# A one-core hybrid decoder layer: the w_o projection with the tokens stationary, its gate and x loaded as rows in its first slab, and five spare buffers for modulation weights in two more stretches

## The chip, the cores and the metric

The kernel runs on one core of one Trainium2 chip. A core has a matrix engine (TensorE, PE in the profile, with its weight loads shown apart as PEld), a vector engine (VectorE, DVE), a scalar engine (ScalarE, ACT), GpSimd (POOL) and SyncE (SP), whose queue issues nearly all DMAs here. The metric is the device time of one execution in microseconds (us), lower is better. The kernel before was timed three times: 1594.55, 1594.61 and 1588.14 us, median 1594.55.

## The reference

One layer (depth 1) for 256 tokens of width 2048, all in float32:

```python
mod = (silu(c) @ ada_w[l] + ada_b[l])[:, None, :]
sh1, sc1, g1, sh2, sc2, g2 = split(mod, 6)              # each 2048 wide
h = modulate(rms_norm(x, norm1_g[l]), sh1, sc1)         # h * (1 + scale) + shift
u, lru_gate, q, k, v, mix_gates = split(h @ w_in[l] + b_in[l])
y_lru  = rg_lru(conv(u)) * gelu(lru_gate)               # 16 heads of 128
y_attn = sliding_window_attention(q, k, v, sinks)       # window 128, 16 q heads, 4 kv heads
merged = sigmoid(g_A) * (y_lru @ w_lru_out[l]) + sigmoid(g_B) * (y_attn @ w_attn_out[l])
x = x + g1 * (merged @ w_o[l])                          # the step that is changed
h2 = modulate(rms_norm(x, norm2_g[l]), sh2, sc2)        # and this one
gate, up = split(h2 @ w_ffn_in[l])                      # 2 x 5632
x = x + g2 * ((silu(gate) * up) @ w_ffn_out[l])
return rms_norm(x, final_g)
```

There is one vector c for all tokens, so each of the six parts of `mod` is one row of 2048 numbers. `ada_w` is 2048 x 12288, 100 MB in float32, a quarter of all that is read.

## The kernel before

**Products.** Every large product is float32 made of three fp32r products (`mm3`, lines 320 to 322): each weight and each activation is cut into a high part (`hi`, fp32r) and the rest (`lo`), and hi·hi, hi·lo and lo·hi are added up in PSUM. Weights come in items of 128 x 1024 (512 KB). An item is loaded by SP into one of five `raw` buffers (line 266), cast to `hi` by ScalarE (line 275, four buffers), and `lo = raw - hi` is made by VectorE (line 287, three buffers). Eight items are a slab: all 2048 input rows by 512 output columns. `step` (line 298) writes item after item: first the post work of finished slabs, then the load of item i+5, `hi` of i+3, `lo` of i+2, the loads of modulation weights, the products of item i, and then side work (lru, attention, modulation) as far as a planner's clock lets it.

**Two forms of a slab** (line 324, `add_slab`). With the weights stationary (`in_rows=False`), one item is 24 matmuls whose moving operand is 256 tokens; the result stands turned, features on the partitions. With the tokens stationary (`in_rows=True`), it is 12 matmuls whose moving operand is 512 weight columns; the result stands in rows, tokens on the partitions. The slabs come in this order: `wi` (u, gate, k, v, q; 14 slabs in pieces), `wgl` (4), `wl` (4), `wga` (4), `wa` (4), `wo` (4), then `fg`/`fu` (11 pairs) and the last product `pf`/`pl`. Only `wi` (but for v) and `wo` have the weights stationary.

**Modulation weights.** Shift, scale and gate 1 and shift and scale 2 are computed by VectorE as dot products (line 407): 158 loads of 512 KB (`aw<-in_ada_t_dram`, line 378), each multiplied by the row `crow` and added up into one column of `modc`, so `modc` holds them turned (128 x 16 for each part). Gate 2 is summed in rows during the first FFN slabs (line 595, 32 loads `aw<-in_ada_g_dram`). `Halves.fetch` has two buffers of its own for these loads (`N_ADA` = 2); when both are taken it may use one of the 25 general buffers `b4` if `spare()` allows. `spare` allows up to five (`N_SPARE`) at the start, and none from the last piece of `wi` on. SP's queue runs in the order in which it was written: a load of modulation weights that waits for its buffer holds all loads behind it.

**w_o and the second norm.** `o_post` adds gate 1 times the product to a turned copy of x (four loads `x1T`, line 120, issued after the first slab), squares it on ScalarE and sums it over features on VectorE. After the fourth slab `second_norm` (line 969) adds up the squares over partitions with ones as weights, takes root and reciprocal over 128 x 256, turns x into rows (32 transposes, line 956), copies the rows out of PSUM on ScalarE and stores them to DRAM (`x1d`, for the last residual), and makes `h2` pair by pair: scaled on VectorE (1001), high part on ScalarE (1005), low part on VectorE (1011).

Of the kernel before, what the change touches and what calls it, by code (L numbers as in the profile page):

```python
# [47 lines left out]

N_PIECES, N_F, K_FIRST = 3, 4, 2
# [16 lines left out]
def hybrid_layer(  # L66
    ctx: ExitStack, tc, vecs, x_t, ada_k, ada_t, ada_g, w_in, bv_row, bm_row, bg_row, lru_w, w_lru, w_att, w_o,
# [37 lines left out]
    def rows(t):  # L105
        return slice(t * P, (t + 1) * P)
# [807 lines left out]
    x1T, second = [], {}  # L914

    def o_post(s):
        def post(banks):
            if s == 0:
                x1T.extend(load_x("x1T"))
                second["fs"] = b4("fs2")  # L920
# [5 lines left out]
            yield 0, 0  # L926
            for f in range(4):
                xf = x1T[s][:, f, :]
                nc.vector.scalar_tensor_tensor(
                    xf, banks[f // 2][:, f % 2, :], modc[:, 2, 4 * s + f:4 * s + f + 1], xf,  # L930
                    op0=ALU.mult, op1=ALU.add,
                )
            yield 1.3, 0
            sq = b4(f"sq{s}")
            nc.scalar.activation(sq, x1T[s], AF.Square)
            yield 0, 0.95
            nc.vector.tensor_reduce(second["fs"][:, s, :], sq.rearrange("p k s -> p s k"), axis=AX.X, op=ALU.add)
            yield 1.14, 0
# [10 lines left out]
    pts = {}  # L949

    def rows_of(i, of_w=False):

        s, t = divmod(i, 2)
        pt = wtile(f"ptx{i}").rearrange("p j n -> p (j n)") if of_w else mtile(f"ptx{i}")
        for j in range(4):
            nc.tensor.transpose(pt[:, j * P:(j + 1) * P], x1T[s][:, j, rows(t)], ident)
        pts[i] = (pt, 0 if of_w else 1)

    def rows_out(i):
        s, t = divmod(i, 2)  # L960
        pt, m = pts.pop(i)
        xr = b4(f"xr{i}", F32, (512,))
        nc.scalar.copy(xr, pt)
        nc.sync.dma_start(x1d[rows(t), s * 512:(s + 1) * 512], xr)
        free(b4=1, m=m)
# [3 lines left out]
    def second_norm(banks):  # L969
        sides[:] = [ada_ffn]  # L970
        fs = second["fs"]
        both = h2["both"] = hp.tile([P, NK, 2, S], F32R, tag="h", name="h2_both")
        hh, hl = both[:, :, 0, :], both[:, :, 1, :]
        ps = mtile("r2_ps")[:, 0:S]
        for s in range(3):
            nc.tensor.matmul(ps, lhsT=ones, rhs=fs[:, s, :], start=s == 0, stop=False, skip_group_check=True)
        sq = b4("sq3")
        for f in range(4):
            xf = x1T[3][:, f, :]
            nc.vector.scalar_tensor_tensor(  # L980
                xf, banks[f // 2][:, f % 2, :], modc[:, 2, 12 + f:13 + f], xf, op0=ALU.mult, op1=ALU.add
            )
            nc.scalar.activation(sq[:, f, :], xf, AF.Square)
        for f in range(4):
            nc.tensor.matmul(ps, lhsT=ones, rhs=sq[:, f, :], start=False, stop=f == 3, skip_group_check=True)
        r2 = b4("r2")[:, 0, :]
        nc.scalar.activation(r2, ps, AF.Sqrt, bias=eps_t, scale=1.0 / D)
        nc.vector.reciprocal(r2, r2)
        free(m=1)

        for i in range(6):
            rows_of(i, i in (3, 4))
        for i in range(4):
            rows_out(i)
            if i < 2:
                rows_of(6 + i)

        def scaled(p):
            for kt in (2 * p, 2 * p + 1):
                xk = x1T[kt // 4][:, kt % 4, :]  # L1000
                nc.vector.scalar_tensor_tensor(xk, xk, modc[:, 4, kt:kt + 1], r2, op0=ALU.mult, op1=ALU.mult)

        def high(p):
            for kt in (2 * p, 2 * p + 1):
                nc.scalar.activation(
                    hh[:, kt, :], x1T[kt // 4][:, kt % 4, :], AF.Identity, bias=modc[:, 3, kt:kt + 1]
                )
# [379 lines left out]
```

## Time and profile before

| what | us |
|---|---|
| three runs | 1594.55, 1594.61, 1588.14 |
| median | 1594.55 |
| the profiled execution | 1595.45 |
| its span, first to last instruction | 1593.7 |
| PE busy in the span | 1568.6 |
| DVE busy | 1126.1 |
| ACT busy | 761.4 |
| `wo` slabs, first to last matmul | 751.1 to 844.0 |

The granted TensorE clock was 0.998. Line numbers (L287) are those of the kernel before. In a row of the timeline the first number is the start, the second the duration; what stands in brackets is the idle time of that engine just before and what ended it. In a row of the waits the numbers are the total, the count and the longest.

### The profile page before, as it was taken

The numbers are of one execution on the slowest core, as the hardware profiler recorded it, in microseconds if no ns is written. First come the engines' busy times: TensorE is split into PE (matmuls) and PEld (weight loads), VectorE is DVE, ScalarE is ACT, GpSimd is POOL, SyncE is SP. The second block draws the span as 40 slices with busy tenths as digits, with TensorE's granted clock in tenths as the row PEclk, the third lists the DMA queues.
The fourth block names the chain that finished last, engine by engine and source line by source line (L and its number), as shares of the span: only waits on it lengthen the run. The fifth ranks groups of instructions, "written<-read, shape, count | busy, mean of one in ns | idle before, by whom it ended". The sixth has DMA issues, their size and how long they took to land.

```text
span 1593.7 us, 22492 instructions
## 1 busy us (share of the span) xinstructions
PE 1568.6 (98%) x8532; PEld 1358.6 (85%) x8532; DVE 1126.1 (71%) x1430; ACT 761.4 (48%) x955; POOL 3.9 (0%) x9
## 2 busy tenths in 40 slices
PE   8999999999999999999999999999999999999997
PEld 7999999998878888777998878888888888888886
DVE  7889989899888888788657877445455444444465
ACT  4644444767845455333446444444444444333343
POOL 0000000000000000000000000000000000000000
PEclk9999999999999999999999999999999999999999
DMA  9999988665877888998766899566666666655553
GB/s 362 355 322 334 347 290 280 242 216 181 302 240 254 299 274 279 327 304 302 283 183 214 305 332 337 174 189 194 185 188 193 186 188 233 231 193 198 191 193 120
DMA packets 112143, 399.36 MB, mean 251 GB/s; under 512 B 12449, under 2 KB 12577, under 8 KB 111649
## 3 DMA queue, kind: packets, MB, share of 16 engines
q1 hardware_dynamic: 111746, 397.40, 73.8%
q8 instruction: 67, 1.10, 0.3%
q10 hardware_dynamic: 288, 0.52, 0.1%
q14 instruction: 42, 0.34, 0.1%
HBM read 393.68 MB, written 4.19 MB: 250 GB/s over the span
## 4 chain that ended last, share of the span: by engine, by line
PE 86%; DMA 9%; DVE 3%; issue 1%; ACT 1%; SPq 0%; DVEq 0%; ACTq 0%
PE pf L1111 11%; PE wi L322 6%; PE wi L321 6%; PE wi L320 6%; PE fg L320 5%; PE fu L321 5%; PE fg L321 5%; PE fu L322 5%; PE fg L322 5%; PE fu L320 5%; DMA aw<-in_ada_t_dram 4%; PE pl L1111 3%; DMA aw<-in_ada_g_dram 2%; PE wo L320 2%; PE wo L321 2%; PE wo L322 2%
## 5 line engine op out<-in xcount | busy, mean ns | idle before, releaser
L275 ACT CAST hi<-raw 128x1024 fp32r<-128x1024 f32 (+1 forms) x540 | 560.4, 1040 | 765.7 <-PE pf L1111 109.8
L287 DVE TENSOR_TENSOR lo<-raw,hi 128x1024 fp32r<-128x1024 f32 (+1 forms) x540 | 648.9, 1206 | 361.6 <-PE pf L1111 95.7
L322 PE MATMUL wi<-h_both,lo 128*128 128x256 f32 x800 | 226.6, 283 | 2.1 <-DVE lo L287 2.1
L320 PE MATMUL wi<-h_both,hi 128*128 128x256 f32 x800 | 227.4, 284 | 1.3 <-ACT acc L496 1.3
L321 PE MATMUL wi<-h_both,hi 128*128 128x256 f32 x800 | 226.4, 283 | 0.0
L322 PEld LDWEIGHTS wi<-h_both,lo 128*128 128x128 f32 x800 | 153.5, 192 | 2.5 <-DVE lo L287 2.5
L320 PEld LDWEIGHTS wi<-h_both,hi 128*128 128x128 f32 x800 | 153.5, 192 | 1.7 <-ACT acc L496 1.5
L321 PEld LDWEIGHTS wi<-h_both,hi 128*128 128x128 f32 x800 | 153.5, 192 | 0.2
L320 PE MATMUL fg<-hi,h_both 128*128 128x512 f32 x352 | 139.1, 395 | 0.0
L321 PE MATMUL fu<-lo,h_both 128*128 128x512 f32 x352 | 137.1, 390 | 1.7 <-DVE lo L287 1.6
L322 PE MATMUL fg<-hi,h_both 128*128 128x512 f32 x352 | 137.1, 389 | 0.0
L321 PE MATMUL fg<-lo,h_both 128*128 128x512 f32 x352 | 137.0, 389 | 0.0
L320 PE MATMUL fu<-hi,h_both 128*128 128x512 f32 x352 | 137.0, 389 | 0.0
L322 PE MATMUL fu<-hi,h_both 128*128 128x512 f32 x352 | 136.9, 389 | 0.0
L407 DVE CUSTOM_DVE_ANT_0 aw<-aw,crow,vec 128x1024 f32<-128x1024 f32 x79 | 100.7, 1277 | 18.3 <-DMA aw<-in_ada_t_dram 18.2
L407 DVE CUSTOM_DVE_ANT_0 aw<-aw,crow,modc 128x1024 f32<-128x1024 f32 x79 | 100.8, 1280 | 15.8 <-DMA aw<-in_ada_t_dram 15.3
L1111 PE MATMUL pf<-hi,fh 128*128 128x512 f32 x264 | 88.5, 389 | 0.0
L1111 PE MATMUL pf<-lo,fh 128*128 128x512 f32 x264 | 88.4, 389 | 0.0
L1111 PE MATMUL pf<-hi,fl 128*128 128x512 f32 x264 | 88.4, 389 | 0.0
L321 PEld LDWEIGHTS fu<-lo,h_both 128*128 128x128 f32 x352 | 66.1, 188 | 16.2 <-DVE lo L287 2.5
L320 PEld LDWEIGHTS fg<-hi,h_both 128*128 128x128 f32 x352 | 66.1, 188 | 14.2 <-issue 0.7
L321 PEld LDWEIGHTS fg<-lo,h_both 128*128 128x128 f32 x352 | 66.1, 188 | 14.0 <-issue 0.7
(232 smaller groups left out, 2567.9 us busy)
## 6 DMA issues: line engine op xcount, KB each, us to landing
raw<-in_w_f_dram SPq DMA_DIRECT2D x176, 512.0 KB, 3.5
raw<-in_w_in_dram SPq DMA_DIRECT2D x164, 512.0 KB, 6.6
aw<-in_ada_t_dram SPq DMA_DIRECT2D x158, 512.0 KB, 5.9
raw<-in_w_f2a_dram SPq DMA_DIRECT2D x44, 512.0 KB, 4.3
raw<-in_w_lru_dram SPq DMA_DIRECT2D x32, 512.0 KB, 6.5
raw<-in_w_att_dram SPq DMA_DIRECT2D x32, 512.0 KB, 7.2
raw<-in_w_o_dram SPq DMA_DIRECT2D x32, 512.0 KB, 4.1
aw<-in_ada_g_dram SPq DMA_DIRECT2D x32, 512.0 KB, 5.5
```

Source lines behind the costliest of these rows:

```text
L275: nc.scalar.copy(hi[:, :cols], live[i][0][:, :cols])
L287: nc.vector.tensor_tensor(lo[:, :cols], raw[:, :cols], f32(hi[:, :cols]), op=ALU.subtract)
L320: nc.tensor.matmul(ps, lhsT=lh, rhs=rh, start=start, stop=False, skip_group_check=True)
L321: nc.tensor.matmul(ps, lhsT=lh, rhs=rl, start=False, stop=False, skip_group_check=True)
L322: nc.tensor.matmul(ps, lhsT=ll, rhs=rh, start=False, stop=stop, skip_group_check=True)
L407: nc.vector.tensor_tensor_reduce(out=r, in0=r, in1=crow[:, j * CH:(j + 1) * CH], op0=ALU.mult, op1=ALU.add, scale=1.0, scalar=dst if j els ...
L1111: nc.tensor.matmul(fin[t, n], lhsT=l[:, rows(t)], rhs=w[:, c0:c0 + 512], start=kt == 0 and k == 0, stop=kt == (EARLY if (t, n) == (1, 3) e ...
```

## The change

Four edits.

1. The four `w_o` slabs are made with the tokens stationary. The product stands in rows; so do x, the residual and the gate that it needs.
2. In the fourth item of the first `w_o` slab (`late` = 6), `w_o_first` loads x in rows (`xr`, 4 x 512 KB, a new input `x_r`), turns the 16 columns of gate 1 by one transposition, writes this row to DRAM (`g1d`, 8 KB) and reads it back into all partitions (`g1`, two loads of 512 KB). The four loads of turned x are gone.
3. The residual is stored as soon as a slab has it (`keep_rows`), the squares are summed along the row by ScalarE's accumulator, the root is taken over 128 x 2, and its reciprocal is spread by two diagonal blocks and one product with ones. The turned x that `h2` needs is made by 32 transpositions: 16 are written before the last residual, 12 after it, 4 after the first FFN item. Two and five small matmuls (`keep_warm`) stand around the product that spreads the root.
4. `spare` allows five more buffers again for modulation weights: for `ada_t` from the last `wl` slab's post work on (if attention is done or has room), and for `ada_g` in the FFN.

```diff
+N_WARM_2 = (2, 5)
...
     def ada_rows():
         got = Halves([ada_g[kt, :, j * CH:(j + 1) * CH] for kt in range(NK) for j in range(2)])
+        got.spare = lambda: len(got.got) - got.own < N_SPARE
...
     def lru_post(s):
             if s == 3:
                 free(b4=8)
+                halves.spare = lambda: len(halves.got) - halves.own < N_SPARE and (
+                    len(at_lo) == 4 or used["b4"] + 4 <= room["b4"]
+                )
...
+    def gate_rows():
+        while not {(2, kt) for kt in range(NK)} <= cols_done:
+            ada.advance(True)
+        ps = mtile("g1_ps")
+        nc.tensor.transpose(ps[0:NK, 0:P], modc[:, 2, :], ident)
+        row = sp.tile([P, S], F32, tag="t2", name="g1_row")
+        nc.scalar.copy(row[0:NK, 0:P], ps[0:NK, 0:P])
+        free(m=1)
+        nc.sync.dma_start(g1d, row[0:NK, 0:P])
+        for i in range(2):
+            g1.append(b4(f"g1{i}", F32, (CH,)))
+            nc.sync.dma_start(
+                g1[i], g1d[8 * i:8 * i + 8, :].rearrange("k p -> (k p)").partition_broadcast(P)
+            )
...
+    def load_rows():
+        for s in range(4):
+            xr.append(b4(f"xr{s}", F32, (2, 512)))
+            nc.sync.dma_start(xr[s], x_r[:, s * 512:(s + 1) * 512].rearrange("(t p) n -> p t n", p=P))
+    def w_o_first():
+        load_rows()
+        gate_rows()
...
     def o_post(s):
-            if s == 0:
-                x1T.extend(load_x("x1T"))
...
-            for f in range(4):
-                xf = x1T[s][:, f, :]
-                nc.vector.scalar_tensor_tensor(
-                    xf, banks[f // 2][:, f % 2, :], modc[:, 2, 4 * s + f:4 * s + f + 1], xf,
...
-            nc.vector.tensor_reduce(second["fs"][:, s, :], sq.rearrange("p k s -> p s k"), axis=AX.X, op=ALU.add)
+            y = b4(f"yo{s}", F32, (2, 512))
+            for t in range(2):
+                nc.vector.tensor_tensor(y[:, t, :], in_rows_of(banks[t]), g1_of(s), op=ALU.mult)
+            yield 1.4, 0
+            nc.vector.tensor_tensor(xr[s], xr[s], y, op=ALU.add)
+            yield 1.13, 0
+            for t in range(2):
+                nc.scalar.activation(y[:, t, :], xr[s][:, t, :], AF.Square, accum_out=ss2[:, t, s:s + 1])
+            keep_rows(s)
...
-        add_slab(w_o[s], f"wo{s}", mact, 0, NK, o_post(s), before=x_first if s == 3 else None)
+        add_slab(w_o[s], f"wo{s}", mact, 0, NK, o_post(s), True, (w_o_first, None, None, x_first)[s], 6 if s == 0 else 0)
...
     def second_norm(banks):
+        for p in range(4):
+            turn(p)
+        y = b4("yo3", F32, (2, 512))
+        for t in range(2):
+            nc.vector.tensor_tensor(y[:, t, :], in_rows_of(banks[t]), g1_of(3), op=ALU.mult)
+            nc.vector.tensor_tensor(xr[3][:, t, :], xr[3][:, t, :], y[:, t, :], op=ALU.add)
+            nc.scalar.activation(y[:, t, :], xr[3][:, t, :], AF.Square, accum_out=ss2[:, t, 3:4])
+            if t == 0:
+                turned_copy(0, nc.scalar.copy)
+        keep_rows(3)
+        turn(4, True)
+        sr = sp.tile([P, 2], F32, tag="rc", name="sr")
+        turned_copy(1, nc.vector.tensor_copy)
+        nc.vector.tensor_reduce(sr, ss2, axis=AX.X, op=ALU.add)
+        nc.scalar.activation(sr, sr, AF.Sqrt, bias=eps_t, scale=1.0 / D)
+        nc.vector.reciprocal(sr, sr)
+        turn(5)
+        turn(6)
+        nc.vector.tensor_scalar(diag[:, rows(0)], ident, sr[:, 0:1], None, op0=ALU.mult)
+        nc.scalar.activation(diag[:, rows(1)], ident, AF.Copy, scale=sr[:, 1:2])
+        keep_warm(N_WARM_2[0], True)
+        nc.tensor.matmul(r2_ps, lhsT=ones, rhs=diag, start=True, stop=True)
+        keep_warm(N_WARM_2[1], True)
...
         def rest():
+            turn(7)
```

Where the instructions stand now. In the rows of SP's queue the names in brackets are what the instruction waits for: `DMAHW` is an earlier DMA of the same rotation, `DVE`, `Activation` and `PE` are an engine that has to be done with the buffer. Line numbers of the change are shifted by two here (L380 is the old L378, L268 the old L266).

First place, SP's queue in the `wa` slabs, where a modulation load (`aw`) stands between weight loads (`raw`). Before:

```order
L378 DMA aw_6691<-in_ada_t_dram 128x1024 [waits DMAHW6_49,DVE_49]
L266 DMA raw_6693<-in_w_att_dram 128x1024 [waits DMAHW7_49,Activation_49]
L378 DMA aw_6712<-in_ada_t_dram 128x1024 [waits DMAHW0_49,DVE_49]
L266 DMA raw_6714<-in_w_att_dram 128x1024 [waits DMAHW1_49,Activation_49]
L266 DMA raw_6733<-in_w_att_dram 128x1024 [waits DMAHW2_49,Activation_49]
L378 DMA aw_6739<-in_ada_t_dram 128x1024 [waits DMAHW3_49,DVE_49]
```

Of the change, the same place:

```order
L380 DMA aw_6690<-in_ada_t_dram 128x1024 [waits DMAHW1_49,DVE_49]
L268 DMA raw_6704<-in_w_att_dram 128x1024 [waits DMAHW2_49,Activation_49]
L380 DMA aw_6710<-in_ada_t_dram 128x1024 [waits DMAHW3_49]
L268 DMA raw_6725<-in_w_att_dram 128x1024 [waits DMAHW4_49,DVE_49]
L380 DMA aw_6731<-in_ada_t_dram 128x1024 [waits DMAHW5_49,DVE_49]
L268 DMA raw_6746<-in_w_att_dram 128x1024 [waits DMAHW6_49,Activation_49]
```

Before, every modulation load waits for VectorE to have used the one two loads earlier; now some of them have a general buffer and wait for no engine, so the loads turn over three buffers and not two. When the `w_att` loads begin, SP has issued 128 modulation loads where it had issued 124, and at the last of them 153 where it had 150.

Second place, SP's queue in the first `w_o` slab of the change; before, weight loads alone stood here, and four loads of turned x after the slab:

```order
L268 DMA raw_7420<-in_w_o_dram 128x1024 [waits DMAHW6_49,DMAHW1_49,DVE_49]
L947 DMA xr_7426<-in_x_r_dram 128x2x512
L947 DMA xr_7428<-in_x_r_dram 128x2x512
L947 DMA xr_7430<-in_x_r_dram 128x2x512
L947 DMA xr_7432<-in_x_r_dram 128x2x512 [waits DMAHW2_49,PE_49]
L928 DMA g1d<-g_row 16x128 [waits DMAHW3_49,Activation_49]
L931 DMA g_7439<-g1d 128x1024 [waits DMAHW4_49,DMAHW3_49]
L931 DMA g_7441<-g1d 128x1024 [waits DMAHW5_49]
L268 DMA raw_7459<-in_w_o_dram 128x1024 [waits DMAHW6_49,DVE_49]
```

The load of item 9 (`raw_7459`) now stands behind seven DMAs, two of which wait: the store of the gate for ScalarE's copy, and the first load of it for that store to have landed.

Third place, VectorE from the end of the last `w_o` slab to the first pair of `h2`. Before:

```order
L980 SCALAR_TENSOR_TENSOR x1T_7616<-wo_0_0_8125,modc,x1T_7616 128x256 x2
L980 SCALAR_TENSOR_TENSOR x1T_7616<-wo_0_1_8126,modc,x1T_7616 128x256 x2
L988 RECIPROCAL r_8386<-r_8386 128x256
L1001 SCALAR_TENSOR_TENSOR x1T_7610<-x1T_7610,modc,r_8386 128x256 x2
L1011 SCALAR_TENSOR_TENSOR h_both<-x1T_7610,modc,h_both 128x256 x2
```

Of the change:

```order
L1013 TENSOR_TENSOR yo_8015<-wo_0_0_7850,g_7441 128x512
L1014 TENSOR_TENSOR xr_7432<-xr_7432,yo_8015 128x512
L1013 TENSOR_TENSOR yo_8015<-wo_0_1_7851,g_7441 128x512
L1014 TENSOR_TENSOR xr_7432<-xr_7432,yo_8015 128x512
L999 COPY x1T_8031<-pt_8000 128x512
L1022 TENSOR_REDUCE sr<-ss_176 128x2
L1024 RECIPROCAL sr<-sr 128x2
L1028 TENSOR_SCALAR yo_8015<-ident,sr 128x128
L1041 SCALAR_TENSOR_TENSOR x1T_8019<-x1T_8019,modc,r_ps 128x256 x2
L1054 SCALAR_TENSOR_TENSOR h_both<-x1T_8019,modc,h_both 128x256 x2
```

The reciprocal over 256 columns is gone; two products, two additions, a copy, a small reduction, a small reciprocal and a diagonal block stand in its place.

More of the change, by code (lines that the diff above doesn't have):

```diff
@@ L913, in hybrid_layer, with keep_rows, g1_of @@
     x1d = dp.tile([S, D], F32, name="x1d")
[L914 removed]
+    xr, x1T, pts = [], {}, {}
+    ss2 = const.tile([P, 2, 4], F32, name="ss2")
+    def load_rows():
[5 more added lines that the diff above has]
+        gate_rows()
+    def keep_rows(s):
+        nc.sync.dma_start(x1d[:, s * 512:(s + 1) * 512].rearrange("(t p) n -> p t n", p=P), xr[s])
+    def g1_of(s):
+        return g1[s // 2][:, s % 2 * 512:(s % 2 + 1) * 512]
     def o_post(s):
         def post(banks):
[L918 to L920 removed]
             if s == 3:
@@ L946, in hybrid_layer, with turn, turned_copy @@
     for s in range(4):
-        add_slab(w_o[s], f"wo{s}", mact, 0, NK, o_post(s), before=x_first if s == 3 else None)
[L949 to L965, printed above, removed]
+        add_slab(w_o[s], f"wo{s}", mact, 0, NK, o_post(s), True, (w_o_first, None, None, x_first)[s], 6 if s == 0 else 0)
+    def turn(p, of_w=False):
+        pt = wtile(f"pt{p}") if of_w else mtile(f"pt{p}").rearrange("p (j n) -> p j n", n=S)
+        for j in range(2):
+            for t in range(2):
+                c = (2 * p + j) % 4 * P
+                nc.tensor.transpose(pt[:, j, rows(t)], xr[p // 2][:, t, c:c + P], ident)
+        pts[p] = (pt, 0 if of_w else 1)
+    def turned_copy(p, eng):
+        pt, m = pts.pop(p)
+        x1T[p] = b4(f"x1T{p}", F32, (2, S))
+        eng(x1T[p], pt)
+        free(m=m)
     h2 = {}
@@ L970, in second_norm @@
         sides[:] = [ada_ffn]
-        fs = second["fs"]
         both = h2["both"] = hp.tile([P, NK, 2, S], F32R, tag="h", name="h2_both")
         hh, hl = both[:, :, 0, :], both[:, :, 1, :]
[L974 to L1001, printed above, removed]
+        for p in range(4):
+            turn(p)
@@ new lines, in second_norm @@
+        y = b4("yo3", F32, (2, 512))
+        for t in range(2):
+            nc.vector.tensor_tensor(y[:, t, :], in_rows_of(banks[t]), g1_of(3), op=ALU.mult)
[6 more added lines that the diff above has]
+        sr = sp.tile([P, 2], F32, tag="rc", name="sr")
@@ new lines, in second_norm, with scaled @@
+        keep_warm(N_WARM_2[0], True)
+        nc.tensor.matmul(r2_ps, lhsT=ones, rhs=diag, start=True, stop=True)
+        keep_warm(N_WARM_2[1], True)
+        def scaled(p, r):
+            if p in pts:
+                (pt, m), x1T[p] = pts.pop(p), b4(f"x1T{p}", F32, (2, S))
+            else:
+                pt, m = x1T[p], 0
+            for j in range(2):
+                nc.vector.scalar_tensor_tensor(
+                    x1T[p][:, j, :], pt[:, j, :], modc[:, 4, 2 * p + j:2 * p + j + 1], r, op0=ALU.mult, op1=ALU.mult
+                )
+            free(m=m)
@@ L1003, in high @@
         def high(p):
[L1004 to L1007, printed above, removed]
+            for j in range(2):
+                kt = 2 * p + j
+                nc.scalar.activation(hh[:, kt, :], x1T[p][:, j, :], AF.Identity, bias=modc[:, 3, kt:kt + 1])
         def low(p):
-            for kt in (2 * p, 2 * p + 1):
+            for j in range(2):
+                kt = 2 * p + j
@@ L1011, in low @@
                 nc.vector.scalar_tensor_tensor(
-                    hl[:, kt, :], x1T[kt // 4][:, kt % 4, :], modc[:, 3, kt:kt + 1], f32(hh[:, kt, :]),
+                    hl[:, kt, :], x1T[p][:, j, :], modc[:, 3, kt:kt + 1], f32(hh[:, kt, :]),
                     op0=ALU.add, op1=ALU.subtract,
@@ L1016, in rest @@
         def rest():
+            turn(7)
             for p in range(NK // 2):
-                if 0 < p < 4:
-                    rows_out(4 + p)
-                for stage, ahead in ((low, 2), (scaled, 3), (high, 3)):
-                    if p + ahead < NK // 2:
-                        stage(p + ahead)
+                if p + 2 < NK // 2:
+                    low(p + 2)
+                if p + 3 < NK // 2:
+                    scaled(p + 3, r2)
+                    high(p + 3)
                 yield 1.33, 1.4
-        scaled(0)
+        scaled(0, r2_ps)
         high(0)
-        rows_out(4)
+        nc.scalar.copy(r2, r2_ps)
         low(0)
-        scaled(1)
+        scaled(1, r2)
         high(1)
         low(1)
-        scaled(2)
+        scaled(2, r2)
         high(2)
```

24 lines of the change are left out of this document (11 added, 13 removed).

## The prediction

> **What bounds the kernel now.** I read the busy times and the chain of waits on the page first, then the stages one by one.
>
> ```profile
> PE 1568.6 (98%) x8532; PEld 1358.6 (85%) x8532; DVE 1126.1 (71%) x1430; ACT 761.4 (48%) x955; POOL 3.9 (0%) x9
> PE 86%; DMA 9%; DVE 3%; issue 1%; ACT 1%; SPq 0%; DVEq 0%; ACTq 0%
> ```
>
> TensorE sets the end: 98% busy and 86% of the chain. Time can be won in two ways: fewer or shorter matmuls, or less idle time of TensorE. The stages (windows; columns: length, busy time of PE, PEld, DVE, ACT, POOL, clock, DMA share, GB/s):
>
> ```profile
> 553.20:652.60 99.40, 98.98 (x441) 80.06 (x440) 82.06 (x131) 49.36 (x73) 0.00 (x0) 1.00 0.87 286
> 652.60:751.10 98.50, 91.93 (x409) 73.93 (x408) 80.54 (x102) 38.21 (x40) 0.00 (x0) 1.00 0.92 310
> 751.10:844.10 93.00, 93.00 (x777) 92.96 (x777) 58.07 (x61) 39.96 (x42) 1.81 (x1) 1.00 0.68 225
> 844.10:850.80 6.70, 6.70 (x48) 6.09 (x47) 3.51 (x5) 3.98 (x10) 0.00 (x0) 1.00 0.24 85
> 850.80:1000.00 149.20, 147.52 (x656) 120.61 (x655) 120.58 (x127) 71.29 (x87) 0.00 (x0) 1.00 0.90 312
> ```
>
> They are, in order, the `wga` slabs, the `wa` slabs, the `wo` slabs, the second norm, and the FFN while gate 2 is computed. TensorE idles 0.4, 6.6, 0, 0 and 1.7 us in them, 8.7 in all. In the second norm it counts as busy, but with reductions and transposes: there a chain through four engines bounds.
>
> Why it idles in `wa` is told by the waits of that window and, last row, of the FFN window:
>
> ```profile
> PE wa L321 <- DVE lo L287: 6.6, 4, 3.0
> DVE aw L407 <- DMA aw<-in_ada_t_dram: 16.6, 14, 2.5
> SPq L378 <- DVE modc L407: 72.9, 26, 4.9
> SPq L378 <- DVE pa L595: 47.3, 30, 5.5
> ```
>
> TensorE waits for `lo`; VectorE made it late because it had waited for a modulation load in front of it; and that load had been issued late, since SP waited on each of the 26 loads until VectorE had used the one two before (2.8 us each). The longest stall in the timeline:
>
> ```profile
> 723.10 0.08 DVE L407 DVE_READ_ACCUMULATOR2_ANT modc<- 128x1 f32 x1
> 723.20 0.33 SPq L378 DMA_DIRECT2D aw<-in_ada_t_dram  x1
> 730.07 1.28 DVE L407 CUSTOM_DVE_ANT_0 aw<-aw,crow,modc 128x1024 f32<-128x1024 f32 x1 [2.41 <-DMA aw<-in_ada_t_dram]
> 732.48 1.21 DVE L287 TENSOR_TENSOR lo<-raw,hi 128x1024 fp32r<-128x1024 f32 x1
> 733.75 0.50 PE L321 MATMUL wa<-lo,oh 128*128 128x512 f32 x1 [3.00 <-DVE lo L287]
> ```
>
> The buffer came free at 723.18, the load went out 0.02 us later, VectorE stood 2.41 us, and TensorE 3.00.
>
> **The change part by part.** *Spare buffers.* Two buffers in rotation bound the rate:
>
> ```profile
> L378 SPq DMA_DIRECT2D aw<-in_ada_t_dram x26: 327/328/328, 653.1 to 750.8; - x26
> DMA to landing us min/median/max: 4.6/5.9/7.1
> ```
>
> A buffer is taken for 5.9 us of landing and 1.28 of use, 7.2; two of them give a load every 3.6 us, and with jitter it was (750.8 - 653.1) / 25 = 3.9. Without stalls the stage would last 98.5 - 6.6 = 91.9 us, and needs one every 3.5. So the buffers bound it. With three in rotation, as the order of SP's queue now has it, the bound is 7.2 / 3 = 2.4, well under 3.5. What is late next is VectorE: 80.54 of 91.9 us would be 88%. That leaves little room, so I let 2.0 of the 8.7 us stay and count -6.7, with -8.7 and 0 as the ends. The FFN has the same rotation (its wait row above), and the spare loads run ahead there from the first slab. `wga` gets four loads more than before, with 286 GB/s used.
>
> *The slabs.* Before: 93.0 us for 768 matmuls and eight transposes of `mt`. 32 transposes take 3.66 us (row below), so eight take 0.9; 92.1 / 768 = 0.120 us each. After: 384 matmuls with 512 columns, as in any `fu` slab without stall:
>
> ```profile
> L320 PE MATMUL fu<-hi,h_both x32: 389/389/389, 872.8 to 893.9; 128*128 128x512 f32 x32
> ...
> L322 PE MATMUL fu<-hi,h_both x32: 389/389/389, 873.2 to 894.3; 128*128 128x512 f32 x32
> ```
>
> 96 matmuls have their first and last start at 872.8 and 894.3: 21.5 / 95 = 0.2263 us, times 384 = 86.9. Gain 5.2, with a tenth to either side for the rounding of the rows. By the Trainium skill, TensorE: Matmul & The Clock Gate, Back-to-back issue gap, a matmul of 256 columns has 262 cycles at 2.4 GHz and one of 512 has 518, which speaks against this edit: 768 x 262 and 384 x 518 cycles differ by 1.0 us only. The trace has 0.120 us where the page has 0.109, so the measurement decides, and by the page the sum below would be 4.2 us higher.
>
> *The second norm.* Before, the last `wo` matmul starts at 844.04 and the first `fg` at 850.83: 6.79 us.
>
> ```profile
> 844.04 0.28 PE L322 MATMUL wo<-mh,lo 128*128 128x256 f32 x1
> 844.36 0.88 DVE L980 SCALAR_TENSOR_TENSOR x1T<-wo,modc,x1T 128x256 f32<-128x256 f32 x2 [0.57 <-PE wo L322]
> 847.18 3.66 PE L956 MATMUL ptx<-ident,x1T 128*128 128x128 f32 x32
> 849.75 0.88 DVE L1001 SCALAR_TENSOR_TENSOR x1T<-x1T,modc,r 128x256 f32<-128x256 f32 x2
> 850.83 0.50 PE L320 MATMUL fg<-hi,h_both 128*128 128x512 f32 x1
> ```
>
> The new chain has its twins at the kernel's end (product, sum, square, small root) and at its start (diagonal, product with ones):
>
> ```profile
> 1579.49 0.69 DVE L1123 TENSOR_TENSOR y<-pl,pa 128x512 f32<-128x512 f32 x1 [1.78 <-PE pl L1111]
> 1580.22 0.69 DVE L1125 TENSOR_TENSOR last<-y,last 128x512 f32<-128x512 f32 x1
> 1582.48 0.75 DVE L1171 SCALAR_TENSOR_TENSOR last<-last,r 128x512 f32<-128x512 f32 x1
> ...
> 16.09 0.40 ACT L1273 ACTIVATE sqx<-ident,rc 128x128 f32<-128x128 f32 x1 [0.82 <-DVE rc L1270]
> 16.70 0.60 PE L1275 MATMUL rx_ps<-sqx,ones 128*128 128x256 f32 x2
> 17.33 0.37 ACT L1278 COPY rx<-rx_ps 128x256 f32<-128x256 f32 x1 [0.84 <-PE rx_ps L1275]
> ```
>
> Let L be the start of the last `wo` matmul. The first token half is done 6 x 0.226 = 1.36 us earlier; its result can be read 0.39 + 0.04 after its start (389 ns above; 0.32 after 0.28 before), at L - 0.93. Product and sum take 1579.49 to 1580.22 and 0.69 more, so the second half's product starts at L + 0.49. From there to a reciprocal in use 2.99 (1579.49 to 1582.48), to the spreading product 0.61, to its reader 0.63, and from the scaling to the first `fg` 1.08 (849.75 to 850.83): L + 5.8. Gain 1.0; ends 0.3 (the copy queued on VectorE between the sums and the reduction gets in the way, priced as a product, 0.69) and 1.3. The 28 transposes and the warm products lie in this gap. Neither form leaves TensorE without work for long there, and the granted clock stayed at 1.00 in this stage.
>
> *Added on the path.* Four transposes after the first FFN item (4 x 3.66 / 32 = 0.46 us) and one for the gate (0.11): +0.6. The residual in rows costs VectorE 2 x 0.69 + 1.21 a slab (1.21 as `lo` in the stall above, of the same size) against 2 x 0.88 and a reduction; it has 58.07 of 93.00 us there, so this is hidden, as is ScalarE's accumulation (39.96 of 93.00). The stores of the residual wait on SP for that sum; three weight items are cut ahead of need at that time, which covers it.
>
> *The gate's round trip.* SP reaches the loads of x once `raw` of item 8 is out. They run while TensorE is in items 1 to 3; the store of the gate waits for TensorE to get to item 3 and for a copy, the first load of the gate for the store, and `raw` of item 9 for both. The nearest rows:
>
> ```profile
> bm<-in_bm_row_dram SPq DMA_DIRECT2D x8, 256.0 KB, 6.4
> x1T<-in_x_t_dram SPq DMA_DIRECT2D x4, 512.0 KB, 6.7
> raw<-in_w_o_dram SPq DMA_DIRECT2D x32, 512.0 KB, 4.1
> L275 ACT CAST hi<-raw 128x1024 fp32r<-128x1024 f32 (+1 forms) x540 | 560.4, 1040 | 765.7 <-PE pf L1111 109.8
> ```
>
> Store about 4.1, then gate and `raw` 9 behind each other in 6.7, about 12 us after TensorE's start of item 3 with 1 us of copying. Item 9 is needed 6 x 2.72 = 16.3 after that start (12 x 0.2263 an item), less 2.3 for `hi` and `lo` (1.04 and 1.21): 14.0. It fits with 2 us. If each of the three takes 6.7, 21.1 us, TensorE stands 7. Behind `raw` 9 wait the next weight loads alone. I take +0.5, ends 0 and 7.
>
> **Sum**, against the profiled execution of 1595.45 (span 1593.7 and 1.75 around it): -6.7 - 5.2 - 1.0 + 0.6 + 0.5 = -11.8, so **1583.7**. The median of the three runs is 0.9 lower than that execution, and one of the three was at 1588.14.
>
> **The rivals.**
> *The wait changes its name.* The spare buffers fill, but weight loads then come late instead, and the 8.7 us stay: 1583.7 + 6.7 = 1590.4. For it: DMA share 0.92 in `wa`. Against it: the same queues moved more at the start, with the same two kinds of load:
>
> ```profile
> 0.00:100.00 100.00, 93.39 (x661) 87.14 (x662) 81.57 (x130) 58.32 (x105) 0.70 (x6) 1.00 0.95 352
> ```
>
> `wa` at full pace asks 30.5 MB (98.5 x 0.310) in 91.9 us, 332 GB/s, under 352. The Trainium skill, DMA: Bandwidth & Descriptors, Specifications, gives about 358 GB/s as a core's share of HBM; by that limit too the stage fits, with 7% to spare, and the trace's 352 agrees with it.
> *The loads collide, and it gets slower.* `wga` and `wa` moved 99.4 x 0.286 + 98.5 x 0.310 = 59.0 MB in 197.9 us, 298 GB/s; the order has two loads more, 60.0 MB. If deeper queues bring the rate down, the loss passes the other parts' 5.1 us where 60.0 MB take over 203.0, below 296 GB/s. At `wga`'s 286 they take 209.8: +11.9 - 5.1, and **1602**. For it: the larger share at a lower rate (0.92 for 310 against 0.95 for 352). Against it: 352.
> *The gate's round trip shows*, the 7 us above with the rest as forecast: 1590.
> *The change doesn't do what it says* could only be for the buffers, if the loads still waited for VectorE; the order of SP's queue shows that some don't, so it has no chance of its own.
>
> **How the numbers follow.** Forecast 0.62 (1583.7, its own range 1580 to 1588), stalls under another name 0.25, the gate's round trip 0.07, collision 0.06. Range: low end 1595.45 - 8.7 - 5.3 - 1.3 + 0.6 = 1580.7, and 2 us less for what varies between runs, 1578.5; high end 1591.5, which takes in 1590. About 0.5% (8 us) is what a measurement of this kernel can tell from no change, so faster means below 1586.6: most of the forecast's share, 0.60. Same: 0.34. Slower: 0.06.
>
> **What would show it.** `wo` from first to last matmul about 87.8 us (93.0); 5.8 us from the last `wo` to the first `fg`; idle time of TensorE in `wa` under 2 us, and SP's wait for `modc` there far under 72.9; no idle row of `wo` around item 9. I am wrong if `raw` takes the place of `aw` as what VectorE and ScalarE wait for and TensorE's idle time stays, or if `wga` begins to stall.

## The result, and the profile after

The changed kernel takes **1579.38 us** (median of six runs, 1578.01 to 1582.76); the kernel before, beside it, 1592.26 (six runs, 1588.14 to 1594.61). The ratio is 0.9924, with a 95% interval of 0.9907 to 0.9940: faster by 12.9 us, where 11.8 were forecast against the profiled execution and 1583.7 as the time. Time and direction lie inside what was forecast, though 1579.38 is 0.6 us under the narrower range, 1580 to 1588, that the forecast had beside its 1583.7. The parts do not all lie inside, and one of them is there only because of another.

The page of the changed kernel, busy times and the chain of waits (profiled execution 1578.05, span 1576.3):

```profile
PE 1559.2 (99%) x8151; PEld 1338.9 (85%) x8151; DVE 1123.1 (71%) x1427; ACT 760.2 (48%) x960; POOL 3.8 (0%) x9
PE 95%; DMA 3%; DVE 1%; ACT 0%; issue 0%; SPq 0%; DVEq 0%; ACTq 0%
```

TensorE's share of the chain rose from 86% to 95%, and that of the DMAs fell from 9% to 3%. The stages, as windows (length, busy time of PE, PEld, DVE, ACT, POOL, clock, DMA share, GB/s): `wga`, `wa`, `wo`, the second norm, the FFN's first part.

```profile
552.70:651.30 98.60, 98.60 (x441) 80.13 (x440) 87.92 (x142) 50.53 (x74) 0.00 (x0) 1.00 0.90 320
651.30:741.00 89.70, 89.70 (x410) 74.54 (x409) 79.17 (x98) 37.64 (x39) 1.81 (x1) 1.00 0.96 332
741.00:828.90 87.90, 87.90 (x394) 72.89 (x393) 49.79 (x47) 40.09 (x49) 0.00 (x0) 1.00 0.70 239
828.90:834.50 5.60, 5.54 (x46) 5.09 (x44) 3.83 (x10) 3.17 (x9) 0.00 (x0) 1.00 0.55 168
834.50:984.00 149.50, 148.99 (x662) 121.88 (x663) 120.48 (x127) 70.54 (x86) 0.00 (x0) 1.00 0.86 297
```

TensorE has no idle time left in `wga`, `wa` and `wo`. From the first matmul of a stage to the first of the next, profile against profile:

| stretch | before | after | difference | forecast |
|---|---|---|---|---|
| up to `wga` | 553.3 | 552.7 | -0.6 | 0 |
| `wga` | 99.3 | 98.6 | -0.7 | buffers, |
| `wa` | 98.5 | 89.7 | -8.8 | -6.7 in all |
| `wo`, first to last matmul | 92.9 | 87.8 | -5.1 | -5.2 + 0.1 + 0.5 |
| last `wo` to first `fg` | 6.8 | 5.7 | -1.1 | -1.0 |
| FFN up to `pf` | 493.6 | 492.6 | -1.0 | +0.5, and its part of -6.7 |

They add up to -17.3. The two profiled executions differ by 17.4, which is 4.5 us more than the medians do: that of before, 1595.45, is slower than all of its six runs, and that of the changed kernel, 1578.05, is 1.3 under its median. Profile against profile the forecast of 11.8 is 5.6 us short, so its nearness to the 12.9 of the medians is in part luck. The -0.6 ahead of `wga` is scatter: the same instructions took 552.6 us in one profile of the changed kernel's form and 555.6 in another.

The waits that stood behind `wa`'s 6.6 us of idle time are gone from TensorE's list. What is left of them in that window:

```profile
DVE aw L409 <- DMA aw<-in_ada_t_dram: 1.8, 4, 0.7
ACT hi L277 <- DMA raw<-in_w_att_dram: 13.4, 7, 2.3
SPq L380 <- DVE modc L409: 35.0, 16, 4.4
```

and, from the view of the loads' line, how long the modulation loads took to land there:

```profile
DMA to landing us min/median/max: 5.8/7.9/9.5
```

VectorE waits 1.8 us for modulation loads where it waited 16.6, and SP 35.0 us for a free buffer where it waited 72.9. A load now takes 7.9 us to land, not 5.9, with more of them under way; TensorE does not feel it, because the load goes out earlier.

### The profile page after: what moved, and what is told of

Read it like the earlier page. It is cut to its first block, busy times and chain, and to the rows that moved or that the text cites. A ratio compares the mean times of both kernels' runs of the same rounds, so it can differ in the third digit from the quotient of the medians.

```text
span 1576.3 us, 21711 instructions
## 1 busy us (share of the span) xinstructions
PE 1559.2 (99%) x8151; PEld 1338.9 (85%) x8151; DVE 1123.1 (71%) x1427; ACT 760.2 (48%) x960; POOL 3.8 (0%) x9
## 4 chain that ended last, share of the span: by engine, by line
PE 95%; DMA 3%; DVE 1%; ACT 0%; issue 0%; SPq 0%; DVEq 0%; ACTq 0%
PE pf L1155 11%; PE wi L324 6%; PE wi L323 6%; PE wi L322 6%; PE fu L322 5%; PE fu L323 5%; PE fu L324 5%; PE fg L324 5%; PE fg L322 5%; PE fg L323 5%; PE pl L1155 3%; PE wga L324 2%; PE wga L323 2%; PE wga L322 2%; PE wo L322 2%; PE wo L323 2%
## 5 line engine op out<-in xcount | busy, mean ns | idle before, releaser
L322 PEld LDWEIGHTS fu<-hi,h_both 128*128 128x128 f32 x352 | 66.1, 188 | 14.1 <-issue 0.5
```

The costliest lines, as they stand in the source:

```text
L322: nc.tensor.matmul(ps, lhsT=lh, rhs=rh, start=start, stop=False, skip_group_check=True)
```

## The experiments

Times are medians with the lowest and highest run; each is compared with runs of the kernel before on the same chip.

### The form of w_o without the spare buffers

```diff
-        got.spare = lambda: len(got.got) - got.own < N_SPARE
...
-                halves.spare = lambda: len(halves.got) - halves.own < N_SPARE and (
-                    len(at_lo) == 4 or used["b4"] + 4 <= room["b4"]
-                )
```

> The change without its fourth edit: no spare buffers in the wga, wa and FFN stages, all else as changed. Theory (the edits add up, and the buffers alone empty the wa stage): wa lasts 98.5 us again with about 6.6 us of TensorE idle time, wo 87.9, 5.7 from the last wo to the first fg; against the kernel before -5.1 - 1.1 + 0.6 = -5.6, so about 1586.7 where before has 1592.3. Rival (the 8.8 us that wa got shorter came partly from the new form of w_o, whose loads and side work stand next to it): wa is well under 98.5, and the time is near 1583. A third, that the new form leans on the buffers (its gate needs 16 columns of modulation early): a stall in the first wo items, wo longer than 88.5.

Measured: 1594.29 (1592.2 to 1595.28, ten runs) beside 1592.4 of before, ratio 1.001 (1.000 to 1.002). Three of the four edits, for which I had counted -5.1 us together, gain nothing without the fourth. The windows of `wga`, `wa`, `wo` and the second norm:

```profile
553.50:654.80 101.30, 99.22 (x441) 79.95 (x440) 81.31 (x131) 49.26 (x73) 0.00 (x0) 1.00 0.83 277
654.80:753.30 98.50, 93.82 (x409) 76.50 (x408) 81.47 (x102) 38.46 (x40) 0.00 (x0) 0.97 0.92 314
753.30:845.90 92.60, 90.15 (x394) 73.97 (x394) 54.26 (x55) 39.93 (x49) 1.81 (x1) 0.98 0.74 251
845.90:851.50 5.60, 5.54 (x46) 5.09 (x44) 3.83 (x10) 3.17 (x9) 0.00 (x0) 1.00 0.54 159
```

`wa` is back at 98.5, `wga` is 2.0 us longer than in the kernel before (more on that in the next experiment), the second norm keeps its gain, and `wo` takes 92.6 us instead of 87.9. The waits in it that name the cause, ScalarE's and SP's:

```profile
ACT hi L277 <- DMA raw<-in_w_o_dram: 19.1, 7, 10.4
SPq L927 <- DMA g1d<-g_row: 6.6, 1, 6.6
```

and the timeline of SP's queue and of the work around item 9 (start, duration, what it waited for):

```profile
761.81 1.96 SPq L943 DMA_DIRECT2D xr<-in_x_r_dram  x4
765.40 0.34 SPq L924 DMA_DIRECT2D g1d<-g_row  x1
772.42 0.83 SPq L927 DMA_DIRECT2D g<-g1d  x2
773.34 8.91 SPq L268 DMA_DIRECT2D raw<-in_w_o_dram  x6
...
778.62 0.39 PE L324 MATMUL wo<-hi,ml 128*128 128x512 f32 x1
779.60 1.04 ACT L277 CAST hi<-raw 128x1024 fp32r<-128x1024 f32 x1 [10.38 <-DMA raw<-in_w_o_dram]
780.70 0.50 PE L322 MATMUL wo<-hi,mh 128*128 128x512 f32 x1 [1.69 <-ACT hi L277]
781.95 0.50 PE L323 MATMUL wo<-lo,mh 128*128 128x512 f32 x1 [0.76 <-DVE lo L289]
783.24 0.63 PE L324 MATMUL wo<-hi,ml 128*128 128x512 f32 x1
```

This is the gate's round trip. The same wait of SP in the changed kernel:

```profile
SPq L931 <- DMA g1d<-g_row: 4.4, 1, 4.4
```

and the same rows of its timeline:

```profile
745.68 1.97 SPq L947 DMA_DIRECT2D xr<-in_x_r_dram  x4
750.60 0.35 SPq L928 DMA_DIRECT2D g1d<-g_row  x1
755.41 0.83 SPq L931 DMA_DIRECT2D g<-g1d  x2
756.33 3.60 SPq L268 DMA_DIRECT2D raw<-in_w_o_dram  x5
762.44 1.05 ACT L277 CAST hi<-raw 128x1024 fp32r<-128x1024 f32 x1 [5.59 <-DMA raw<-in_w_o_dram]
763.52 1.23 DVE L289 TENSOR_TENSOR lo<-raw,hi 128x1024 fp32r<-128x1024 f32 x1 [3.95 <-ACT hi L277]
```

With spare buffers SP enters `wo` ahead: x's rows go out 4.7 us after the first `wo` matmul (741.0), without them 8.5 us after it (753.3). The store of the gate stands behind x's 2 MB, and SP waited 6.6 us for it instead of 4.4. So `hi` of item 9 begins 21.5 us after the first matmul with them and 26.3 without. The item is due 25.5 after it (from the 108 matmuls and the transpositions before it): with the spare buffers its `lo` is ready 2.0 us early; without them its first matmul starts 1.85 us late and its second, which needs `lo`, 2.9.

Those 2.9 us are not the whole loss of 4.7 in `wo`. The last row has a duration of 0.63 where a matmul takes 0.39: seven or eight matmuls behind the stall start 0.43 us apart instead of 0.227, and cost 1.75 more. More on that below.

### The round trip taken off SP's queue

The kernel of the first experiment with the store and the two loads of the gate on GpSimd's queue:

```diff
-        nc.sync.dma_start(g1d, row[0:NK, 0:P])
+        nc.gpsimd.dma_start(g1d, row[0:NK, 0:P])
...
-            nc.sync.dma_start(
+            nc.gpsimd.dma_start(
                 g1[i], g1d[8 * i:8 * i + 8, :].rearrange("k p -> (k p)").partition_broadcast(P)
```

> The change without spare buffers (as in the first experiment), but the store of the gate's row and the two loads that read it back are issued by GpSimd's queue instead of SP's, so that no load of weights stands behind them. In the first experiment TensorE stalled 2.08 + 1.26 us before item 9 of w_o, and the next eight matmuls ran at half the granted clock (8 x 0.2 us): wo took 92.5 us. Theory (SP's wait for the round trip is what took the form's gain away): wo 87.9, no wait for raw of w_o over 3 us, and the time 4.5 us under the first experiment's 1594.3, about 1589.8. Rival (the loads of x in rows are what is in the way, they stay in front of raw 9): raw 9 is still late, wo 89 to 92, time 1591 to 1594. Rival (noise between executions made the first experiment's other stages long): wo 87.9 but the time the same as there.

Measured: 1590.03 (1583.76 to 1594.59, ten runs) beside 1592.15, ratio 0.9979 (0.9963 to 0.9995); 4.3 us under the first experiment. `wa` and `wo`:

```profile
654.40:753.40 99.00, 93.09 (x409) 75.20 (x409) 81.96 (x103) 38.59 (x41) 0.00 (x0) 0.98 0.93 314
753.40:841.40 88.00, 88.00 (x393) 72.77 (x393) 54.69 (x55) 40.11 (x50) 3.52 (x4) 1.00 0.76 265
```

`wo` is at 88.0 us and without idle time, so the wait of SP for the round trip was what took the form's gain in `wo` away; x's rows alone are not in the way. One thing I expected did not come: ScalarE still waits up to 4.8 us for a `raw`, yet not long enough to stop TensorE.

Not the whole gain is back: the kernel is 2.1 us faster than before, where the three edits were expected to give 5.6 in the first experiment. One place is `wga`. From its first matmul to the first of `wa` it lasts 101.3 us in the first experiment's profile and 101.4 in this one, against 99.3 before, with stalls of 1.9 and 1.0 us near 645 us. Yet up to `wo` the instructions of SP, VectorE and ScalarE are the same, in the same order, as in the kernel before. What made these stalls longer is open.

### The spare buffers without the new form

```diff
+        got.spare = lambda: len(got.got) - got.own < N_SPARE
...
+                halves.spare = lambda: len(halves.got) - halves.own < N_SPARE and (
+                    len(at_lo) == 4 or used["b4"] + 4 <= room["b4"]
+                )
```

> The kernel before with the fourth edit alone (spare buffers in the last wl slab's post work and in the FFN). Theory: wa 89.7 us and TensorE without idle time there, wo 93.0 as before, 6.8 to the first fg, the FFN 1.5 to 1.7 shorter: -8.8 - 1.6 - 0.6 = -11, about 1581.3 to 1583 where before has 1592.3. Rival (as forecast, 2.0 of 8.7 us stay; the rest that was seen came from elsewhere): -6.7, about 1585.6, wa about 92.

Measured: 1582.96 (1582.35 to 1583.39, four runs) beside 1592.4, ratio 0.9935 (0.9918 to 0.9952): -9.4 us. Windows of `wga`, `wa`, `wo` and the FFN:

```profile
552.90:651.50 98.60, 98.60 (x441) 80.09 (x440) 86.78 (x140) 50.31 (x74) 0.00 (x0) 1.00 0.90 319
651.50:741.20 89.70, 89.70 (x410) 74.53 (x409) 79.05 (x98) 37.66 (x39) 1.81 (x1) 1.00 0.95 332
741.20:834.20 93.00, 93.00 (x777) 93.00 (x776) 53.16 (x53) 39.76 (x41) 0.00 (x0) 1.00 0.61 198
840.90:1332.20 491.30, 491.30 (x2200) 406.26 (x2201) 289.35 (x279) 218.34 (x242) 0.00 (x0) 1.00 0.70 227
```

`wa` has the changed kernel's length, so its 8.8 us are the buffers' alone. Apart, the form brings +1.9 and the buffers -9.4; together -12.9. Of the 5.4 us between, 4.3 are the round trip, which the buffers hide. The rest may be the longer stalls in `wga`, which are gone with the buffers (98.6 us), or what the medians vary; that was not told apart.

### Which buffers, and how many

One spare buffer instead of five in the two new places:

```diff
-        got.spare = lambda: len(got.got) - got.own < N_SPARE
+        got.spare = lambda: len(got.got) - got.own < 1
```

(and the same in `lru_post`).

> As changed, but with one spare buffer instead of five in the two new places, so three in rotation. Theory (three in rotation bound a load at 7.2/3 = 2.4 us, or at the 9.2 us that landing and use take in the changed kernel at 9.2/3 = 3.1, under the 3.5 us that the stage needs): wa 89.7 to 90.5, the time within 1 us of the changed kernel, 1579.4. Rival (what helps is the lead that several buffers give against jitter of the landing): TensorE idles 2 us or more in wa, and the time is 1581.5 to 1583.

Measured: 1579.67 (1577.14 to 1582.38), ratio 0.9916 (0.9891 to 0.9941). `wa` has 89.70 of 89.70 us busy. Three in rotation are enough, and the other four add nothing that can be measured.

The changed kernel without the spare buffers of the FFN (the line of `got.spare` taken out), and the kernel before with those of `wga` and `wa` alone (the lines of `halves.spare` put in):

> As changed, without spare buffers in the FFN (those for wga and wa stay). Theory after the first experiment (whose FFN, without any spare buffer, took 492.6 us from first fg to first pf as the changed kernel's does): the FFN's spare buffers are worth nothing, FFN 492.6, time as changed, within 0.5 us. As forecast (the 1.7 us of idle time in the FFN of before are those buffers'): FFN 494, time 1.5 us higher.

> The kernel before with spare buffers in wga and wa alone, none in the FFN. Theory (the buffers of the FFN are worth nothing in either form; the 1.8 us stall at 939 us in the profiled execution of before is one that comes and goes): FFN from first fg to first pf 491.3 us as with them, time as with both, 1583.0, within 0.5. As forecast (without them the FFN of before idles 1.7 us): FFN 493 to 494, time 1584.7.

Measured: 1580.03 (1578.06 to 1580.15), ratio 0.9918 (0.9903 to 0.9933), and 1583.71 (1583.43 to 1585.6), ratio 0.9958 (0.9942 to 0.9974). The FFN of each:

```profile
836.60:1329.20 492.60, 492.15 (x2205) 406.72 (x2206) 290.31 (x279) 216.57 (x239) 0.00 (x0) 1.00 0.70 222
```

```profile
842.70:1334.10 491.40, 491.40 (x2202) 406.34 (x2202) 289.49 (x279) 217.92 (x242) 0.00 (x0) 1.00 0.72 227
```

They are as long as with spare buffers (492.6, and 491.4 from the first `fg` to the first `pf`). The times are 0.6 and 0.7 us above those expected, just outside the 0.5 that was allowed. The second kernel gains 7.2 us on the kernel before beside it (1590.91), where with the FFN's buffers it was 9.4; the intervals of the two overlap, and by the stages the FFN gives no reason for the difference, so I take it as scatter of the medians, which no run settles. The stall of 1.8 us that the profile of before has at 939 us is in one of five profiled executions with two buffers and no spare ones in the FFN; it comes and goes, and what sets it off is open.

The opposite, one buffer of its own and no spare one (`N_ADA` = 1 in the kernel before):

> The kernel before with one buffer for modulation loads instead of two (from the last piece of wi on there is no spare one). The planner then asks for a load every two items (5.4 us) in wga and wa and leaves 16 loads for a forced finish in the last w_o slab. Theory (landing plus use, divided by the buffers, bounds the rate): the loads in wga and wa follow each other at 5.9 + 1.3 = 7.2 us or more, wga and wa together last 64/2 x 7.2 = 230 us instead of 198, with a stall of about 1.8 us at nearly every load; the forced finish adds 16 x 7.2 less what else is done there. Time 1680 to 1750. Rival (the rate is the DMA engines', not the buffers'): with fewer loads at a time each lands in 3.5 us or less, the period is 5.4, and wga and wa last 198 us. Of the clock: if a stall of 1.8 us is enough to halve the granted clock for 3.4 us behind it, most stalls are followed by eight matmuls of 0.43 us; if the place of the stall in time decides, some are and some are not.

Measured, a single run: 1703.77. The time is in the range, but not for the reason given. The loads of `wga` and `wa` landed in 4.4 us (below, the view of the loads' line for `wga` and `wa`, then for `wo`), and `wga` and `wa` took 198.6 us, the rival's figure: the planner had put their loads far enough apart. Most of the loss is in `wo`, where what was put off is forced out one by one: 185.6 us, with TensorE idle for 82.7 at one place. Another 15.9 us are lost in the FFN, whose loads have one buffer too.

```profile
DMA to landing us min/median/max: 3.7/4.4/6.6
...
DMA to landing us min/median/max: 3.6/3.8/5.7
```

The window of `wo`:

```profile
750.90:936.50 185.60, 97.06 (x776) 95.98 (x775) 90.22 (x113) 40.28 (x42) 1.80 (x1) 0.77 0.57 189
```

There (second row above) a load lands in 3.8 us, and in the long idle stretch one goes out every 5.2. So the rule (landing and use, divided by the buffers: 3.8 + 1.28 = 5.1) stands, and my figure for landing was wrong: it is no constant, but came out higher the more was under way, 3.8 us alone, 4.4 with weights between, 5.9 with two buffers, 6.8 with one spare one, 7.9 with up to five.

### The small matmuls and the turned rows

Without the two and five small products around the one that spreads the root (`N_WARM_2 = (0, 0)`):

> As changed, without the two and five small products that stand around the product that spreads the root. Theory (they fill idle time of TensorE in a chain that other engines set; the granted clock is 1.00 with or without): 5.7 us from the last wo to the first fg, same time, within 0.5 us. Rival (without them the clock falls, or the product that spreads the root gets slower): the FFN's first matmuls show a lower granted clock, and the time rises by 1 us or more. Other rival (they stand in the way): the gap shortens by 0.1 to 0.3 us.

Measured: 1578.77 (1578.03 to 1581.33), ratio 0.9912 (0.9893 to 0.9931); 5.7 us from the last `wo` to the first `fg`, clock 0.997. They do nothing that can be measured.

The last four transpositions after the third FFN item:

```diff
-            turn(7)
             for p in range(NK // 2):
+                if p == 2:
+                    turn(7)
```

> As changed, but the last four transpositions stand after the third FFN item instead of the first. Theory (after the first item they wait for a PSUM bank that VectorE frees by scaling a pair, and this costs 0.66 us of idle TensorE at 838 us): no gap over 0.5 us there, FFN from first fg to first pf 492.0 instead of 492.6, time 0.6 us under the changed kernel's, within what can be told. Rival (they are then late for the pair that needs them, and h2's last pair comes late): a stall of 0.5 us or more at items 6 or 7 of the first FFN slab, same time or slower.

Measured: 1579.37 (1578.01 to 1580.34), ratio 0.9916 (0.9901 to 0.9931). The FFN takes 491.9 us instead of 492.6, as expected; the wait that goes is this one of the changed kernel (0.50 us idle in the row, 0.66 by the starts of the matmuls around it):

```profile
838.08 0.66 PE L993 MATMUL pt<-ident,xr 128*128 128x128 f32 x4 [0.50 <-DVE x1T L1041]
```

In the time it can't be told: a stall at 459 us with the slower clock behind it took more in the profiled execution than the 0.7 us.

### Three buffers of its own

```diff
-AHEAD, N_HI, N_LO, N_ADA, N_B4 = 6, 4, 3, 2, 25
+AHEAD, N_HI, N_LO, N_ADA, N_B4 = 6, 4, 3, 3, 24
```

with the late transpositions of the experiment above.

> As changed, with three buffers of its own for modulation loads (and 24 general ones instead of 25), and the last four transpositions after the third FFN item. It aims at the stall in the first wl slab, 1.1 to 2.0 us at 458 us in all kernels so far, two times followed by half the granted clock for 3.4 us: there a modulation load waits 8.8 us for VectorE in front of the weights' loads, and no spare buffer is allowed. Theory (the same rotation of two): the stall goes, with 1.5 to 3 us, and the turned rows' 0.66 us with it: 1576.5 to 1578 where the changed kernel has 1579.4. Rival (the stall is there because VectorE itself is late with lo, and the load's wait is only its sign): the stall stays, time 1579.

Measured: 1578.11 (1576.63 to 1579.27), ratio 0.9917 (0.9902 to 0.9931), at the upper end of what was expected. The stall at 458 us is gone from the profile, with 0.7 us at 467 in its place. Once more, beside the changed kernel on one chip:

> The changed kernel itself, beside the kernel with three own buffers and the late transpositions on one chip. Both theories: 1579.4, within 1.

> The kernel with three own buffers and the late transpositions once more, beside the changed kernel on one chip. Its profiled execution had no stall at 458 us (1.1 to 2.0 us before) and none at 838 us (0.66). Theory: 1.5 to 2.5 us under the changed kernel's median. Rival (what was gained there is lost again behind it, as the turned rows' 0.6 us could not be told either): within 0.7 us of it.

Measured: 1578.29 (1577.92 to 1580.05) for the changed kernel, ratio 0.9905 (0.9889 to 0.9921), and 1576.97 (1576.07 to 1581.10) with three buffers, ratio 0.9898 (0.9881 to 0.9914). Again no stall there in its profile, but 1.3 us between the medians lies between the two theories, and is less than the runs of either kernel are apart. Whether it is faster stays open.

## Why the prediction was right, and where it was wrong

**Spare buffers, -6.7: mis-sized.** In the profiles they are worth -9.5, all of it in `wga` and `wa` (-0.7 and -8.8), and nothing in the FFN, whose 1.7 us I had counted in; the medians gave -9.4 with all of them and -7.2 without the FFN's. Three steps failed. First, "ends -8.7 and 0" took the idle time of TensorE for all that could be won. Counted from matmul start to matmul start, `wa`'s four stalls cost 7.2 us, not 6.6, since the 0.39 us of the matmul ahead hide 0.16 of each; and 15 smaller delays, four of them right behind the stalls, cost 1.6, of which 0.3 is left. That is 8.5 of the 8.8. Second, the 2.0 us that I let stay because VectorE would be 88% busy did not stay: it is busy for 79.17 of 89.70 us, and TensorE never waits for it. A busy share near 90% was no reason by itself to expect stalls, as VectorE has two items of lead there. Third, the FFN's idle time was read from one execution and is not the buffers'.

**The slabs, -5.2: right** (-5.1), wherever no stall covers it: `wo` took 87.8 us from first to last matmul, as said. The cycles of the Trainium skill, TensorE: Matmul & The Clock Gate, Back-to-back issue gap, would have left 1.0 us of gain. They do not hold for this kernel's 256-column matmuls, which took 0.120 us each and not 0.109; that section gives them for isolated matmuls and says itself that at small sizes they leave out the weight load.

**The second norm, -1.0: right** (-1.1). Its chain, from the last `wo` matmul to the product that spreads the root, its reader and the first `fg`:

```profile
828.81 0.39 PE L324 MATMUL wo<-hi,ml 128*128 128x512 f32 x1
829.24 0.69 DVE L1013 TENSOR_TENSOR yo<-wo,g 128x512 f32<-128x512 f32 x1
831.97 0.17 DVE L1024 RECIPROCAL sr<-sr 128x2 f32<-128x2 f32 x1 [0.36 <-ACT sr L1023]
832.63 0.70 PE L1032 MATMUL r_ps<-yo,ones 128*128 128x256 f32 x2
833.37 0.87 DVE L1041 SCALAR_TENSOR_TENSOR x1T<-x1T,modc,r_ps 128x256 f32<-128x256 f32 x2 [0.91 <-PE r_ps L1032]
834.50 0.50 PE L322 MATMUL fg<-hi,h_both 128*128 128x512 f32 x1
```

834.50 - 828.81 = 5.69, forecast 5.8. The twins from the kernel's start and end priced each link to about 0.2 us: 0.43 to the second half's product (forecast 0.49), 3.39 from there to the spreading product (3.60), 0.74 to its reader (0.63) and 1.13 to the first `fg` (1.08).

**Added on the path, +0.6: too low.** The four transpositions cost 0.46 as counted, but they also make TensorE stand 0.66 us, for a PSUM bank that VectorE was still reading, a wait that I had not named: the FFN without it takes 491.9, with it 492.6, and 491.4 in the old form with the spare buffers.

**The gate's round trip, +0.5 (ends 0 and 7): the size held, the condition was missed.** It is hidden in the changed kernel, with 2.0 us to spare, as "it fits with 2 us" said. But I worked it out as if SP stood where it stands in the kernel before, and added it to the others as a term of its own. With SP there, the trip costs 4.3 us (1594.29 against 1590.03) and the whole form is worth nothing. The four edits are not a sum: the spare buffers give the lead that the round trip uses up.

**The sum.** The stages as measured, -9.5 - 5.1 - 1.1 and +1.2 in the FFN, make -14.5. The medians said -12.9, and -14.0 in the last comparison (1578.29 beside 1592.32), so the stages account for the gain within what the medians vary. What the profiles differ by beyond it, up to -17.3, is the -0.6 of scatter and 2.2 us that the FFN of before took longer in its one profile, its stall among them.

**The rivals.** "The wait changes its name" is refuted: nothing stalls TensorE in `wa`, and the rate there is 332 GB/s, the figure worked out for full pace. The 358 GB/s that the prediction had beside it are no ceiling in these traces: over 1 us the first experiment moved 414 and 410 (last section). "The loads collide" is refuted too: 320 and 332 GB/s, well over 296. "The gate's round trip shows" is what happens without the buffers, and there alone.

## What to carry to other kernels

Price a stall by the spacing of matmul starts in a stretch with it and one without, not by the idle column: here a stretch's loss was a third larger than its idle time. Before adding up the terms of a change, ask for each which queue position it assumes; a round trip through DRAM on a shared queue cost nothing or nearly the whole gain of a stage here, by 4 us of lead. A transfer that has to wait for another one goes better on a queue on which nothing else stands behind it: that was worth 4.3 us without the spare buffers, and was not tried with them.

## What was not expected of the hardware

A stall can cost more than it lasts. Windows of 1 us behind the stall of 2.49 us at 662.9 in the first experiment (the clock is the third number from the end), and then the one behind the longest stall of the kernel before, 3.15 us:

```profile
663.00:664.00 1.00, 1.00 (x3) 0.86 (x4) 0.45 (x1) 0.95 (x1) 0.00 (x0) 0.62 1.02 414
664.00:665.00 1.00, 1.00 (x4) 0.72 (x4) 1.00 (x3) 0.23 (x1) 0.00 (x0) 0.50 1.04 410
```

```profile
733.70:735.00 1.30, 1.25 (x5) 1.05 (x6) 1.30 (x2) 0.00 (x0) 0.00 (x0) 1.00 0.73 233
```

Behind the shorter one the granted clock is 0.50 for some 3.4 us, eight matmuls 0.43 us apart, 1.75 us lost; behind the longer one it stays at 1.00. In the profiles of these runs, and before matmuls of 512 columns, stalls of 1.93, 2.03, 2.39, 2.43, 2.47, 2.49 and 3.51 us were followed by it, while others of 1.93, 2.07, 2.14, 2.18 and 3.15 were not, and none under 1.9 was, but for the pair of 1.85 and 1.03. So the length alone doesn't decide.

The traces speak for the place in time. In each of them every change of the clock lies a whole number of steps of 3.413 us from every other: in the first experiment the slow stretches begin at 663.23, 734.91 and 782.70 us, 21 and 14 steps apart, and each lasts one step. Below are the steps around two stalls of 1.93 us. The first, from 457.1 to 459.0 in the kernel with the late turned rows, lies inside one step; the second, from 1019.5 to 1021.4 in the kernel with one buffer, is cut by a border at 1020.04:

```profile
456.75:460.16 3.41, 1.64 (x8) 1.04 (x7) 3.41 (x5) 2.90 (x3) 0.00 (x0) 1.00 1.07 374
460.16:463.57 3.41, 3.41 (x10) 2.63 (x9) 3.34 (x8) 1.05 (x1) 0.00 (x0) 0.50 0.94 300
```

```profile
1020.04:1023.45 3.41, 2.02 (x9) 1.68 (x10) 2.56 (x3) 2.10 (x2) 0.00 (x0) 1.00 0.66 162
1023.45:1026.86 3.41, 3.41 (x17) 2.75 (x15) 1.89 (x2) 0.55 (x1) 0.00 (x0) 1.00 0.93 317
```

TensorE is busy for 1.64 of 3.41 us in the first and the clock halves in the next step; in the second it is busy for 2.02 and the clock stays. How much idle time in a step it takes is open, though: the stall of 2.18 us lies all but 0.1 us inside one step, and was not followed. The Trainium skill, TensorE: Matmul & The Clock Gate, Part 1 on the clock gate, tells of a window of about 3.4 us that runs free and sets the clock to half after an idle one. The steps and the length of the slow stretch agree; but a window need not be idle throughout, since 1.93 us of stall were enough. No run here set the place on purpose.

This price of a stall may be part of why the kernels with stalls spread more from run to run (1588.9 to 1596.2 for before beside the first experiments) than those without (1582.35 to 1583.39 with the buffers alone); that link was not tested.
